# A hybrid residual block in one kernel: wider projections and attention outcome, fill without shared places, four gates moved to the dense stage

## The chip, the cores and the metric

The kernel runs on one core of a Trainium2 chip. The metric is the device time of one execution in microseconds (us): the median of three runs. TensorE is called PE here, VectorE DVE, ScalarE ACT, GpSimd POOL and SyncE SP.

## The reference

One layer on 1024 tokens of 1024 channels in float32. A normed input goes through one projection that is cut into an HGRN2 mixer (4 heads of 128), a forgetting attention (8 heads of 64), a cross attention into 256 memory tokens, and three sigmoid gates of 1024 channels. Each mixer is projected, gated and summed; an output projection and a residual follow, then a convolutional GLU.

```python
h = _rmsnorm(x, norm_mix_g[l])
z = h @ w_in[l]
(hq, hf, hi, hg, fq, fk, fv, ff, mq, gate_logits) = jnp.split(z, pts, axis=-1)
y_a = _hgrn2_mixer(hq, hf, hi, hg, lower_bounds[l], hgrn_norm_g[l])
y_b = _fox_mixer(fq, fk, fv, ff, fox_f_bias[l], fox_q_norm_g[l], fox_k_norm_g[l])
y_c = _memory_mixer(mq, mem_kv, mem_q_norm_g[l], mem_k_norm_g[l])
gates = jax.nn.sigmoid(gate_logits).reshape(B, T, N_BRANCH, D_MODEL)
merged = (gates[:, :, 0] * (y_a @ w_br_hgrn[l]) + gates[:, :, 1] * (y_b @ w_br_fox[l])
          + gates[:, :, 2] * (y_c @ w_br_mem[l]))
x = x + merged @ w_out[l]
x = x + _conv_glu_ffn(_rmsnorm(x, norm_ffn_g[l]), ffn_w_up[l], ffn_conv_w[l], ffn_conv_b[l], ffn_w_down[l])
```

The attention, for a block of 128 queries, with `Fc` the running sum of log forget gates (q and k are normed per head):

```python
s = (jnp.einsum('bhqd,bhkd->bhqk', qh[:, :, lo:hi], kh[:, :, :hi]) * scale
     + Fc[:, :, lo:hi, None] - Fc[:, :, None, :hi])
p = jax.nn.softmax(jnp.where(mask, s, -jnp.inf), axis=-1)
outs.append(jnp.einsum('bhqk,bhkd->bhqd', p, vh[:, :, :hi]))
```

## The kernel before

Every float32 operand of a dense product is split in a high and a low part: `split` (L166 and L174) casts to a rounded format on ACT (`wh`, `ph`) and subtracts on DVE (`wl`, `pl`), and `mm3` (L160 to L162) issues three matmuls: high with high, high with low, low with high.

The stages, in order of time in the profile. The first stage norms x and makes the first gates. The dense stage (to about 205 us) computes pairs of gates by a scheme of seven products instead of eight: 84 matmuls of 512 columns for each of 7 pairs, against 48 matmuls for a gate alone. `NCOVER`, `NPAIR` and `NFOX` say which gates of `ORDER` are made where: in the first stage, as pairs, or beside the attention. A gate goes out to `gd` in DRAM and comes back as `gt` where its branch is projected. Then come attention's values and the memory attention (to 318 us), the attention (to 680), HGRN with its first score matmul at 701, the branches (from about 880), the output projection, the up projection (from 1062) and the down projection (1490 to the end).

Attention, `fox_attn(p, i)`, takes head 2p+i. It loads the head's row of bias, spread over all partitions, into `nf` (one buffer, a DMA on SP). For each of eight tiles of 128 queries POOL makes a masked piece `nfm` (L919); PE makes scores `lg` (L924 and L925) in blocks of up to 512 keys; DVE adds the bias, leaves the sum in `pt` and the maximum in `st` (L930, and small steps on `st` at L935, L937 and L939); ACT takes the exponential (L940), DVE the reciprocal (L941), POOL normalises (L942). After every two tiles the outcome follows: PE transposes 128 by 128 pieces of both tiles into `tr` (L953 to L956, two banks), `split` makes `ph` and `pl`, and PE multiplies them with the split values `vhl` into `po` (L965 and L966), 256 columns wide. ACT and DVE add the halves of `po` (L969, L970) and SP stores them.

Beside it runs dense work, called the fill here: `fox_proj(p+1)` and `hgrn_values`, which call `token_major` with 256 columns (L160 to L162 with `pp<-wh,uh`, 256 columns), and ten gates (`gates_early`, `cm_chunk`, `pp<-uh,wh`, 512 columns). `weave` interleaves generators by their counts of steps, and `ahead` gives the attention's instructions a priority; the final order on each engine is set when the program is built, by a scheduler with a timeline of its own. Weights come as `raw` through SP, in `wp`, three buffers of each of `wh` and `wl`.

`hgrn_prep(h)` projects what a head of HGRN needs (`cm_chunk`, `gt` or `zt` at L1046, `ha`, `L`, `Gt`) and `hgrn_mix` starts from operands `kE`, `X` and `Xk`. `branch(br, yh, yl)` projects a mixer's output; before branch 0 eight DMAs on POOL's queue load the memory mixer's split output `yc`. At the start of the up projection the second norm's scale `rt` is made (sums on PE at L1416, a scalar step on DVE at L178, a power on POOL at L179) and spread by transposes (L366).

## Time and profile before

| what | value |
|---|---|
| median of 3 runs | 1699.6 us (1698.56 to 1700.24) |
| the profiled execution | 1700.23 us, its span 1698.4 us |
| mean granted PE clock | 0.999 |
| busy, PE / weight loads / DVE / ACT / POOL | 1691.0 / 1452.4 / 1150.8 / 800.9 / 324.6 us |
| instructions | 24291 |
| DMA | 227.16 MB, mean 134 GB/s |

A row of a group reads: line, engine, operation, out<-in, count, busy us, mean ns of one, and the idle time ahead of them with what ended it. A row of the timeline begins with the start and the busy time in us. PE's names `pp`, `lg`, `tr` and `po` stand for its banks of PSUM.

### The profile page before, as it was taken

The numbers are of one execution on the slowest core, as the hardware profiler recorded it, in microseconds if no ns is written. First come the engines' busy times: TensorE is split into PE (matmuls) and PEld (weight loads), VectorE is DVE, ScalarE is ACT, GpSimd is POOL, SyncE is SP. The second block draws the span as 40 slices with busy tenths as digits, with TensorE's granted clock in tenths as the row PEclk, the third lists the DMA queues.
The fourth block names the chain that finished last, engine by engine and source line by source line (L and its number), as shares of the span: only waits on it lengthen the run. The fifth ranks groups of instructions, "written<-read, shape, count | busy, mean of one in ns | idle before, by whom it ended". The sixth has DMA issues, their size and how long they took to land.

```text
span 1698.4 us, 24291 instructions
## 1 busy us (share of the span) xinstructions
PE 1691.0 (100%) x8957; PEld 1452.4 (86%) x8957; DVE 1150.8 (68%) x2057; ACT 800.9 (47%) x1428; POOL 324.6 (19%) x420
## 2 busy tenths in 40 slices
PE   9999999999999999999999999999999999999999
PEld 7888899989898998888888888888888888888887
DVE  6966455666666664886856845987878888775654
ACT  6734455545454553775631333644434444533432
POOL 0200032543433331544310000311111111100000
PEclk9999999999999999999999999999999999999999
DMA  9443232221212111110346542566544344494772
GB/s 367 157 161 106 88 139 68 77 92 51 94 59 77 63 46 57 67 32 13 106 127 209 167 186 100 165 174 169 158 139 138 118 149 143 172 363 145 251 269 87
DMA packets 83062, 227.16 MB, mean 134 GB/s; under 512 B 9712, under 2 KB 12408, under 8 KB 82816
## 3 DMA queue, kind: packets, MB, share of 16 engines
q1 hardware_dynamic: 64320, 160.54, 26.8%
q0 software_dynamic: 18048, 64.50, 13.2%
q8 instruction: 70, 1.15, 0.3%
q10 hardware_dynamic: 576, 0.59, 0.1%
q14 instruction: 48, 0.39, 0.1%
HBM read 180.72 MB, written 67.93 MB: 146 GB/s over the span
## 4 chain that ended last, share of the span: by engine, by line
PE 99%; DVE 0%; ACT 0%; DMA 0%; issue 0%; ACTq 0%; DVEq 0%
PE pp L160 21%; PE pp L162 21%; PE pp L161 21%; PE lg L160 4%; PE lg L162 4%; PE lg L161 4%; PE tr L162 3%; PE tr L161 3%; PE tr L160 3%; PE po L966 1%; PE lg L925 1%; PE lg L924 1%; PE po L965 1%; PE po L160 1%; PE po L161 1%; PE po L162 1%
## 5 line engine op out<-in xcount | busy, mean ns | idle before, releaser
L160 PE MATMUL pp<-uh,wh 128*128 128x512 f32 x412 | 163.3, 396 | 0.0
L161 PE MATMUL pp<-ul,wh 128*128 128x512 f32 x412 | 162.9, 395 | 0.0
L162 PE MATMUL pp<-uh,wl 128*128 128x512 f32 x412 | 162.5, 394 | 0.0
L161 PE MATMUL pp<-wl,uh 128*128 128x256 f32 (+1 forms) x512 | 146.3, 286 | 0.0
L162 PE MATMUL pp<-wh,ul 128*128 128x256 f32 (+1 forms) x512 | 146.1, 286 | 0.0
L160 PE MATMUL pp<-wh,uh 128*128 128x256 f32 (+1 forms) x512 | 145.6, 286 | 0.0
L166 ACT CAST wh<-s 128x512 fp32r<-128x512 f32 x110 | 66.5, 621 | 131.6 <-PE pp L161 55.1
L166 ACT CAST wh<-raw 128x1024 fp32r<-128x1024 f32 (+2 forms) x76 | 67.6, 890 | 100.6 <-PE pp L161 86.2
L166 ACT CAST wh<-rw 128x512 fp32r<-128x512 f32 x87 | 53.2, 619 | 108.1 <-PE pp L161 70.2
L160 PEld LDWEIGHTS pp<-wh,uh 128*128 128x128 f32 x512 | 97.3, 190 | 1.2
L161 PEld LDWEIGHTS pp<-wl,uh 128*128 128x128 f32 x512 | 97.4, 190 | 1.0
L162 PEld LDWEIGHTS pp<-wh,ul 128*128 128x128 f32 x512 | 97.4, 190 | 0.9
L1457 POOL DMA_DIRECT2D rw<-in_w_up x44 | 24.1, 555 | 372.4 <-DVE wl L1350 171.3
L166 ACT CAST dwh<-wr 128x1024 fp32r<-128x1024 f32 (+1 forms) x41 | 40.2, 980 | 115.8 <-PE tr L161 40.0
L162 PEld LDWEIGHTS pp<-uh,wl 128*128 128x128 f32 x412 | 77.5, 188 | 15.1
L174 DVE TENSOR_TENSOR wl<-raw,wh 128x1024 fp32r<-128x1024 f32 (+2 forms) x75 | 78.0, 1040 | 17.8 <-ACT wh L166 17.6
L160 PEld LDWEIGHTS pp<-uh,wh 128*128 128x128 f32 x412 | 77.5, 188 | 14.6
L161 PEld LDWEIGHTS pp<-ul,wh 128*128 128x128 f32 x412 | 77.5, 188 | 14.5
L940 ACT ACTIVATE pt<-pt,st 128x128 f32<-128x128 f32 (+3 forms) x64 | 49.7, 777 | 41.7 <-DVE st L937 33.9
L174 DVE TENSOR_TENSOR dwl<-wr,dwh 128x1024 fp32r<-128x1024 f32 (+1 forms) x41 | 46.3, 1129 | 31.7 <-ACT dwh L166 31.7
L942 POOL TENSOR_SCALAR pt<-pt,st 128x128 f32<-128x128 f32 (+3 forms) x64 | 49.1, 767 | 78.4 <-DVE st L941 64.1
L1350 DVE TENSOR_TENSOR wl<-rw,wh 128x512 fp32r<-128x512 f32 x69 | 47.7, 704 | 22.7 <-PE pp L162 18.2
(500 smaller groups left out, 5123.2 us busy)
## 6 DMA issues: line engine op xcount, KB each, us to landing
rw<-in_w_up POOLq DMA_DIRECT2D x44, 512.0 KB, 4.7
sd<-in_w_dn POOLq DMA_DIRECT2D x30, 512.0 KB, 6.0
br<-yd SPq DMA_DIRECT2D x30, 512.0 KB, 5.0
raw<-in_w_cm SPq DMA_DIRECT2D x24, 512.0 KB, 3.4
gd<-gt SPq DMA_DIRECT2D x48, 256.0 KB, 2.0
gt<-gd SPq DMA_DIRECT2D x48, 256.0 KB, 2.7
yd<-fc SPq DMA_DIRECT2D x44, 256.0 KB, 2.2
wr<-sd SPq DMA_DIRECT2D x20, 512.0 KB, 4.5
```

Source lines behind the costliest of these rows:

```text
L160: PE.matmul(ps, lh, rh, start=first, stop=False, skip_group_check=more)
L161: PE.matmul(ps, lh, rl, start=False, stop=False, skip_group_check=more)
L162: return PE.matmul(ps, ll, rh, start=False, stop=last, skip_group_check=more)
L166: return S.copy(out, in_)
L174: return (sub or V).tensor_sub(l, src, h.bitcast(F32))
L924: PE.matmul(ps[:, :w], qa[i][:, tsl], kh[i][:, s0:s0 + w], start=True, stop=False)
L925: fox_sets[p][3] = PE.matmul(ps[:, :w], qa[i][:, tsl], kl[i][:, s0:s0 + w], start=False, stop=True)
L940: S.activation(pt[:, :ns], pt[:, :ns], AF.Exp, bias=st[:, 2:3], accum_out=st[:, 3:4])
L942: G.tensor_scalar(pt[:, :ns], pt[:, :ns], st[:, 3:4], 0.0, ALU.mult, ALU.add)
L965: PE.matmul(o, vhl[:, sb, :], ph[:, src], start=(sb == 0), stop=False)
L1350: late["split"] = V.tensor_sub(l, src, h.bitcast(F32))
L1457: late["raw"] = G.dma_start(raw[:, 2 * i:2 * i + 2, :], src[:, 2 * i:2 * i + 2, :])
```

## The change

Nine parts:

1. `NPAIR` goes from 10 to 14: the dense stage makes nine pairs instead of seven, and the attention's fill six gates instead of ten.
2. The query-key projections of the last two head pairs become one of 512 columns (`fox_proj_late`), its result stored to `zd` in DRAM as it comes, and read back and normed by `fox_load`. HGRN's values become one projection of 512 columns as well, stored to `hid` and read back behind attention. The evacuation uses `gate_tile` in place of `Vf` and `z`.
3. The outcome takes groups of four tiles: four transposes fill a bank, and a matmul is up to 512 columns wide. Each tile's `pt` has its own place (`pt0` to `pt7`).
4. The addition of the last head's last `po` (`late["tail"]`) moves into `hgrn_prep(0)`.
5. The weave's counts of steps and what is woven with which head.
6. `wp` has four buffers instead of three (`WIDE`).
7. The loads of `yc` are spread over branch 0, each behind a small POOL instruction that waits for a gate's load.
8. The first unit of the up projection loads by SP; another part of it loads behind a mark on POOL.
9. The scratch for DMA descriptors is set to 2048 bytes.

```diff
-NCOVER, NPAIR = 2, 10
+NCOVER, NPAIR = 2, 14
-NFOX = [0, 3, 0, 3, 0, 3, 1]
+NFOX = 6
+WIDE = 4
...
-            hl = [wp.tile([P, 4 * 264], F32R, tag=t, name=t, bufs=3) for t in ("wh", "wl")]
+            hl = [wp.tile([P, 4 * 264], F32R, tag=t, name=t, bufs=WIDE) for t in ("wh", "wl")]
...
+    def fox_proj_late():
+        def evac(tb, ps):
+            t = gate_tile()
+            S.activation(t, ps, AF.Copy, scale=rt[:, tb:tb + 1])
+            SP.dma_start(zd[tb], t)
+        yield from token_major(w_late[0], HB, evac)
+
+    def fox_load(p):
+        cs = slice((p - 2) * 256, (p - 1) * 256)
+        for n in range(2):
+            z = fox_tile(p, n)
+            SP.dma_start(z, zd[4 * n:4 * n + 4, :, cs].rearrange("b p c -> p b c"))
+            fox_norm(z)
+            yield
...
-        for tp in range(4):
+        for g in range(2):
             pts = []
-            for j in range(2):
-                tb = 2 * tp + j
+            for tb in range(4 * g, 4 * g + 4):
...
-                pt = pf.tile([P, T], F32, tag="pt", name="pt", bufs=4)
+                pt = pf.tile([P, ns], F32, tag=f"pt{tb}", name=f"pt{tb}")
...
-            for sp in range(tp + 1):
+            for sb in range(4 * g + 4):
                 ptr = ps_tr()
...
+                first = max(sb - 4 * g, 0)
+                for j in range(first, 4):
+                    PE.transpose(ptr[:, j * P:(j + 1) * P], pts[j][:, sb * P:(sb + 1) * P], ident)
...
+                c = slice(first * P, HB)
+                split(S, ph[:, c], pl[:, c], ptr[:, c])
+                PE.matmul(po[:, c], vhl[:, sb, :], ph[:, c], start=sb == 0, stop=False)
+                PE.matmul(po[:, c], vhl[:, sb, :], pl[:, c], start=False, stop=sb == 4 * g + 3)
                 yield
...
+            if (h, g) == (7, 1):
+                late["tail"] = po, ybd[a, p, g * HB:(g + 1) * HB]
+                return
...
+    late_proj = fox_proj_late()
+    first = (fox_proj(1), chain(islice(late_proj, 4), fox_load(2)), gates_early(1))
+    second = (chain(gates_early(1), islice(late_proj, 4)), gates_early(2), gates_early(1))
     for p in range(3):
-        weave((ahead(fox_attn(p, 0), AHEAD), FOX_STEPS), (fox_proj(p + 1), 8))
+        weave((ahead(fox_attn(p, 0), AHEAD), FOX_STEPS), (first[p], (8, 6, 4)[p]))
         fox_prep(p + 1, fox_sets[p][3])
-        weave((ahead(fox_attn(p, 1), AHEAD), FOX_STEPS), (gates_early(NFOX[2 * p + 1]), 2 * NFOX[2 * p + 1], FOX_LATE))
+        weave((ahead(fox_attn(p, 1), AHEAD), FOX_STEPS), (second[p], 6, FOX_LATE),
+              *([(fox_load(3), 2, 0.1)] if p == 1 else []))
...
     for i in range(2):
-        weave((ahead(fox_attn(3, i), AHEAD), FOX_STEPS), (islice(values, 8), 8),
-              (gates_early(0 if i else NFOX[6]), 2 * NFOX[6], FOX_LATE))
+        weave((ahead(fox_attn(3, i), AHEAD), FOX_STEPS), (chain(gates_early(1 - i), islice(values, 4)), 6 - 2 * i))
...
-    run_all(hgrn_prep(0))
+    for i, _ in enumerate(hgrn_prep(0)):
+        if i == 2:
+            fox_out(gate_tile()[:64, :], *late.pop("tail"))
...
-    for c in range(4):
-        for t, d in zip(yc, ycd):
-            with tc.issue_after(state["norm"].ins):
-                G.dma_start(t[c], d[:, c, :].bitcast(F32R))
-    run_all(branch(0, yh, yl))
+    for i, _ in enumerate(first_branch):
+        if i % 3 and i < 12:
+            p, c = i % 3 - 1, i // 3
+            mark = G.tensor_scalar(warm, late["gates"][:, 0:1], 1.0, 0.0, ALU.mult, ALU.add)
+            with tc.issue_after(mark.ins):
+                G.dma_start(yc[p][c], ycd[p][:, c, :].bitcast(F32R))
...
-            late["raw"] = G.dma_start(raw[:, 2 * i:2 * i + 2, :], src[:, 2 * i:2 * i + 2, :])
+            with tc.issue_after(late["pool"].ins) if after else nullcontext():
+                late["raw"] = (SP if begun else G).dma_start(raw[:, 2 * i:2 * i + 2, :], src[:, 2 * i:2 * i + 2, :])
...
-    nc = bacc.Bacc("TRN2", target_bir_lowering=False, num_devices=1)
+    nc = bacc.Bacc("TRN2", target_bir_lowering=False, num_devices=1, dynamic_dma_scratch_size=2048)
```

Line numbers move: L160 to L162 of before are L161 to L163 of the new program, the scores L954 and L955, the transposes L980, the outcome L985 and L986.

The change moves instructions on every engine. The first place is the end of attention on PE, before: the last outcome group of head 7 (`po`) with the rows around it; `pp` is a dense product.

```order
L966 MATMUL po<-pl,vhl 128x256
L965 MATMUL po<-ph,vhl 128x256
L966 MATMUL po<-pl,vhl 128x256
L953 MATMUL tr<-ident,pt 128x128 x2
L954 MATMUL tr<-ident,pt 128x128 x2
L953 MATMUL tr<-ident,pt 128x128
L956 MATMUL tr<-ident,pt 128x128
L954 MATMUL tr<-ident,pt 128x128
L965 MATMUL po<-ph,vhl 128x256
L966 MATMUL po<-pl,vhl 128x256
L965 MATMUL po<-ph,vhl 128x256
L966 MATMUL po<-pl,vhl 128x256
```

Some twenty rows of `pp` stand ahead of these, and twenty more between them and the last `po` rows. In the new program the same place, from the last scores of head 7 (`lg`, of its eighth tile) to the first transposes of its second group of four tiles:

```order
L954 MATMUL lg<-kh_3_5661,qa_3_5663 128x512
L955 MATMUL lg<-kl_3_5665,qa_3_5663 128x512
L980 MATMUL tr<-ident,pt_6545 128x128
L980 MATMUL tr<-ident,pt_6558 128x128
L985 MATMUL po<-ph,vhl 128x512
L986 MATMUL po<-pl,vhl 128x512
L985 MATMUL po<-ph,vhl 128x384
L980 MATMUL tr<-ident,pt_6558 128x128
L986 MATMUL po<-pl,vhl 128x384
L985 MATMUL po<-ph,vhl 128x256
L986 MATMUL po<-pl,vhl 128x256
L980 MATMUL tr<-ident,pt_6642 128x128
```

No `pp` row stands there, nor anywhere between the first transposes of head 5's first group and the last `po` of head 7; all of the fill stands ahead.

The second place is DVE's queue at the end of attention. Before, with `gt<-pp` and `wl<-raw` the fill's work:

```order
L174 TENSOR_TENSOR pl<-tr,ph 128x384
L1046 TENSOR_TENSOR gt<-pp,rx 128x512
L970 TENSOR_TENSOR yp<-po,yp 64x256
L174 TENSOR_TENSOR pl<-tr,ph 128x512 x2
L174 TENSOR_TENSOR wl<-raw,wh 128x1024
L174 TENSOR_TENSOR pl<-tr,ph 128x512
L174 TENSOR_TENSOR pl<-tr,ph 128x384
L970 TENSOR_TENSOR yp<-po,yp 64x256
```

In the new program:

```order
L929 TENSOR_TENSOR yp<-po,yp 64x512
L175 TENSOR_TENSOR pl<-tr,ph 128x512 x5
L175 TENSOR_TENSOR pl<-tr,ph 128x384
L175 TENSOR_TENSOR pl<-tr,ph 128x256
L175 TENSOR_TENSOR pl<-tr,ph 128x128
L1074 TENSOR_TENSOR gt<-pp,rx 128x512
```

The last splits of attention now stand without the fill's work between them, and the evacuation of a dense product that PE has done earlier (`gt<-pp`) stands behind them all.

The third place is the start of the up projection on PE. Before, the transposes that spread `rt` stand behind the products of `B22` and `T3`:

```order
L161 MATMUL pp<-T3l_10857,wh_10869 128x512
L162 MATMUL pp<-T3h_10856,wl_10870 128x512
L366 MATMUL tr<-ident,rt_10790 128x128 x8
L160 MATMUL pp<-B11h_10175,wh_11004 128x512
L161 MATMUL pp<-B11l_10176,wh_11004 128x512
```

In the new program:

```order
L162 MATMUL pp<-T2l_9746,wh 128x512
L163 MATMUL pp<-T2h_9745,wl_10333 128x512
L161 MATMUL lg<-B22h_10420,wh_10337 128x512
L367 MATMUL tr<-ident,rt_10356 128x128 x8
L162 MATMUL lg<-B22l_10421,wh_10337 128x512
```

They have moved up to behind the first matmul of `B22`, seven matmuls behind the sums from which `rt` is made.

More of the change, by code (lines that the diff above doesn't have):

```diff
@@ L577, in operand @@
             if self.half is None:
-                self.half = [wp.tile([P, 4 * 264], F32R, tag=t, name=t, bufs=3) for t in ("wh", "wl")]
+                self.half = [wp.tile([P, 4 * 264], F32R, tag=t, name=t, bufs=WIDE) for t in ("wh", "wl")]
                 h, l = (t[:, :HB] for t in self.half)
@@ L706, in token_major @@
         with tc.issue_after(late["load"].ins):
-            w = [weights(src[q], (4, ncol)) for q in range(2)]
+            per = 2 if ncol == HB else 4
+            w = [weights(src[q], (per, ncol)) for q in range(KC // per)]
         for tb in range(8):
@@ L1287, in branch @@
                 gts.append(gt)
+            late["gates"] = gts[0]
             for n, ps in br_chunk(br, j, yh, yl):
@@ L1360, in first_operands @@
         a11, a21, a22, a12 = raw
-        h = [wp.tile([P, 4 * 264], F32R, tag="wh", name="wh", bufs=3) for _ in range(2)]
-        sums = [wp.tile([P, 4 * 264], F32R, tag="wl", name="sums", bufs=3).bitcast(F32) for _ in range(2)]
+        h = [wp.tile([P, 4 * 264], F32R, tag="wh", name="wh", bufs=WIDE) for _ in range(2)]
+        sums = [wp.tile([P, 4 * 264], F32R, tag="wl", name="sums", bufs=WIDE).bitcast(F32) for _ in range(2)]
         s1, s2, s4 = sums[0][:, :HB], sums[0][:, HB:2 * HB], sums[1][:, :HB]
@@ L1504, in families @@
                 for k in range(4):
-                    late["last"] = family_block(name, k, quarters(k)[q], G if name == "B21" and k > 1 else None)
+                    sub = G if name == "B21" and k > 1 else None
+                    late["pool" if sub else "last"] = family_block(name, k, quarters(k)[q], sub)
             if name == "T3":
@@ L1776, in pieces @@
         return out
[L1778 removed]
     o["w_fqk"] = c(np.stack([pieces(np.concatenate([fk[:, p * P:(p + 1) * P], fq[:, p * P:(p + 1) * P]], axis=1),
[L1780 removed]
+                                    [(0, 256)])[0] for p in range(2)]))
+    late = np.concatenate([m[:, p * P:(p + 1) * P] for p in (2, 3) for m in (fk, fq)], axis=1)
+    o["w_late"] = c(np.stack([kmaj(m).reshape(P, 4, 2 * HB).transpose(1, 0, 2) for m in (late, hi)]))
     pv = pieces(np.concatenate([fv, ff], axis=1), [(0, 256), (256, 520)])
```

83 lines of the change are left out of this document (38 added, 45 removed).

## The prediction

> **What bounds the kernel now.** I read the page's busy line and its chain first, then PE's waits, then busy time by window, then single groups and the timeline around the places that the change touches.
>
> ```profile
> span 1698.4 us, 24291 instructions
> PE 1691.0 (100%) x8957; PEld 1452.4 (86%) x8957; DVE 1150.8 (68%) x2057; ACT 800.9 (47%) x1428; POOL 324.6 (19%) x420
> PE 99%; DVE 0%; ACT 0%; DMA 0%; issue 0%; ACTq 0%; DVEq 0%
> PE lg L160 <- ACT uh L349: 1.8, 1, 1.8
> PE tr L265 <- POOL dull L263: 1.0, 1, 1.0
> PE po L1189 <- DVE St L1195: 0.7, 1, 0.7
> PE pp L162 <- DVE wl L1350: 0.2, 1, 0.2
> ```
>
> PE is busy throughout, is 99% of the chain, and waits four times in the whole program, 3.7 us together, mostly at the start. So every matmul removed is time gained, and every wait that PE newly meets is time lost; nothing else counts. The profiled execution took 1700.2 us (1.8 us outside its span), 0.6 us over the median of 1699.6. A difference of 0.2%, 3.4 us, is about what a measurement of this kernel can tell from none.
>
> The columns of the next rows are the window in us, then busy time and count of PE, weight loads, DVE, ACT and POOL, then the granted clock, DMA share and GB/s.
>
> ```profile
> 5.00:10.00 5.00, 3.70 (x10) 2.76 (x11) 4.46 (x12) 3.48 (x8) 0.00 (x0) 0.73 1.04 395
> 100.00:200.00 100.00, 100.00 (x443) 82.81 (x442) 51.91 (x82) 38.51 (x68) 3.94 (x8) 1.00 0.27 95
> 600.00:680.00 80.00, 80.00 (x538) 73.39 (x537) 43.06 (x140) 35.52 (x72) 19.27 (x30) 1.00 0.17 54
> ```
>
> 100 to 200 is the dense stage of gate pairs, 600 to 680 the end of attention. There DVE has 43 us of work in 80 because dense matmuls (the fill) stand between attention's own. That is the cover at stake.
>
> **PE's work.** The pitch of a matmul, start to start, is read from runs of equal ones in the timeline:
>
> ```profile
> 1201.63 0.39 PE L160 MATMUL pp<-T4h,wh 128*128 128x512 f32 x1
> ...
> 1202.99 0.39 PE L160 MATMUL pp<-T4h,wh 128*128 128x512 f32 x1
> 599.80 0.28 PE L160 MATMUL pp<-wh,uh 128*128 128x256 f32 x1
> ...
> 601.00 0.28 PE L161 MATMUL pp<-wl,uh 128*128 128x256 f32 x1
> ```
>
> Six steps in 1.36 us give 0.227 us for 512 columns, ten in 1.20 give 0.120 for 256. One wide matmul is thus 0.013 us cheaper than two narrow ones. By instruction counts of both programs the change takes away 992 matmuls of 256 columns and 32 of 128, and adds 456 of 512 and 32 of 384. With 0.17 for 384 (an estimate, halfway between the two pitches) and 0.09 for 128 (an estimate, below the 0.120): -992 x 0.1195 = -118.5, +456 x 0.2267 = +103.4, +32 x 0.17 = +5.5, -32 x 0.09 = -2.9, in all **-12.5 us**. By part: four gates leave the fill with 48 matmuls each and come back as two pairs of 84 in the dense stage, 24 x 0.227 = -5.4; the late query-key and HGRN-value projections go from 768 narrow to 384 wide, -4.7; the outcome matmuls of eight heads are the other 2.4.
>
> The Trainium skill, "TensorE: Matmul & The Clock Gate", section "Back-to-back issue gap", gives an isolated matmul 262 cycles for 256 columns and 518 for 512 at 2.4 GHz, so that widening would save 2.5 ns on a pair. By it the 384 pairs of the projections give 1 us and not 4.7. The trace shows 13 ns on a pair, so I keep 4.7.
>
> **The fill, and what is left bare.** Beside attention, from its first scores to its last outcome matmul, before has 868 narrow and 611 wide fill matmuls: 868 x 0.1195 + 611 x 0.2267 = 242 us. The new program has 105 and 816: 198 us. What decides is where they stand. In PE's new order no fill row stands behind the first transposes of head 5's outcome: its transposes and outcome, and most of heads 6 and 7, follow bare, 224 matmuls, 108 of them transposes of 0.108, 72 outcome and 44 score matmuls; at these pitches 33.0 us. In before, fill stands to the last outcome group. So for these 33 us PE moves as fast as the softmax does, whose work goes on DVE:
>
> ```profile
> L174 DVE TENSOR_TENSOR pl<-tr,ph 128x512 fp32r<-128x512 f32 x48 | 32.2, 684 | 12.0 <-ACT ph L166 11.8
> L174 DVE TENSOR_TENSOR pl<-tr,ph 128x384 fp32r<-128x384 f32 x32 | 17.6, 549 | 1.4 <-ACT ph L166 1.3
> L930 DVE CUSTOM_DVE_ANT_0 pt<-lg,nf 128x512 f32<-128x512 f32 x32 | 22.0, 689 | 20.8 <-PE lg L925 10.8 <-PE tr L953 9.7
> L930 DVE CUSTOM_DVE_ANT_0 pt<-lg,nf 128x384 f32<-128x384 f32 x16 | 8.8, 552 | 1.5 <-PE lg L925 1.4
> L930 DVE CUSTOM_DVE_ANT_0 pt<-lg,nf 128x256 f32<-128x256 f32 x16 | 6.7, 418 | 5.4 <-PE tr L953 4.0 <-PE lg L925 1.3
> L930 DVE CUSTOM_DVE_ANT_0 pt<-lg,nfm 128x128 f32<-128x128 f32 x64 | 18.2, 285 | 13.2 <-POOL nfm L919 7.0 <-PE lg L925 2.8 <-PE po L965 2.0
> L930 DVE DVE_READ_ACCUMULATOR2_ANT st<- 128x1 f32 x144 | 11.8, 82 | 0.0
> L937 DVE TENSOR_SCALAR st<-st 128x1 f32<-128x1 f32 x56 | 11.6, 207 | 0.8
> L941 DVE RECIPROCAL st<-st 128x1 f32<-128x1 f32 x64 | 10.3, 160 | 27.4 <-ACT pt L940 26.8
> L970 DVE TENSOR_TENSOR yp<-po,yp 64x256 f32<-64x256 f32 x32 | 13.2, 412 | 13.1 <-ACT yp L969 12.9
> 655.26 0.55 DVE L930 CUSTOM_DVE_ANT_0 pt<-lg,nf 128x384 f32<-128x384 f32 x1
> 655.73 0.09 DVE L930 DVE_READ_ACCUMULATOR2_ANT st<- 128x1 f32 x1
> 655.73 0.29 DVE L930 CUSTOM_DVE_ANT_0 pt<-lg,nfm 128x128 f32<-128x128 f32 x1
> ```
>
> DVE has 145 instructions in the bare stretch. Those that weigh: 18 splits of 512 (12.3), 6 of 384 (3.3), 12 narrower ones (5.0), the masked sums with maximum (8 x 0.69, 4 x 0.55, 4 x 0.42, 17 x 0.285: 14.2), 33 accumulator reads (2.7), 36 small steps (6.7), 5 additions of the outcome and one value split (2.7): 47 us. The last three rows show that a following instruction starts some 0.08 us ahead of the end of the one before, and that an accumulator read costs nothing of its own; 33 x 0.08 for the reads and about 100 x 0.08 for the rest leave 36.5. So the new wait has a floor of 36.5 - 33 = 3.5, with 1.5 at the entry **5 us**, and 47 - 33 = **14 us** where nothing overlaps.
>
> Neither bound counts latencies. At the last tile of a head (1024 columns) the chain of before runs so:
>
> ```profile
> 658.34 0.21 DVE L937 TENSOR_SCALAR st<-st 128x1 f32<-128x1 f32 x1
> 658.65 1.15 ACT L940 ACTIVATE pt<-pt,st 128x1024 f32<-128x1024 f32 x1 [1.71 <-DVE st L937]
> 659.70 0.18 ACT L940 ACTIVATION_READ_ACCUMULATOR pt<-pt,st 128x1 f32 x1
> 659.92 0.16 DVE L941 RECIPROCAL st<-st 128x1 f32<-128x1 f32 x1 [1.37 <-ACT pt L940]
> 660.25 1.12 POOL L942 TENSOR_SCALAR pt<-pt,st 128x1024 f32<-128x1024 f32 x1 [6.18 <-PE tr L956]
> L166 ACT CAST ph<-tr 128x512 fp32r<-128x512 f32 x48 | 27.1, 588 | 24.9 <-PE tr L954 16.9 <-PE po L965 7.4
> nf<-negFd SPq DMA_DIRECT2D x8, 512.0 KB, 3.7
> ```
>
> That is 3.0 us from the maximum to the normalised tile; ahead of it lie the last scores' latency (0.3), two sums (0.55 and 0.29) and the three-way maximum (0.19), and in the new DVE order two splits and two small steps of the outcome of the group before (1.3): 5.7, with hops between engines about 6.5 us. PE's new order leaves 2.2 us of work (head 6) and 2.7 (head 7) between those scores and the transposes that need the tile, where before never leaves under 6.7. So two waits of about 4 us, **8 us**. The other waits are in the loop over key blocks: two transpose banks go round in 0.32 + 0.26 (latency) + 0.59 (cast) + 0.68 (split) + 0.13 = 2.0 us, against 2 x (4 x 0.108 + 2 x 0.227) = 1.77 of PE, and DVE does sums in between; and a head's first tile waits for the reload of its one row buffer, 3.7 us by the last row. I followed both queues by hand with these durations, each instruction from the latest of its queue, its data and its bank: PE is late by 1.5 us at head 5's second group, 3.9 at head 6's first, 8.1 at its second, 11.1 at head 7's first, 15.2 at its second, 17.8 at the end. Between 14 and 17.8 I take **16 us**, bounds 5 and 25 (half again on the walk).
>
> **Behind attention.**
>
> ```profile
> 694.65 0.68 DVE L1166 TENSOR_TENSOR kE<-kE,kt 128x512 f32<-128x512 f32 x1
> 698.87 0.68 DVE L1098 TENSOR_TENSOR X<-X,hq 128x512 f32<-128x512 f32 x1
> 701.01 0.89 PE lg L1102 x8
> ```
>
> The last outcome matmul of before is at 679.7. HGRN's first operand is ready at 695.3, 15.6 us later; PE had 17.5 us of fill for it, and has 12.2 in the new order: about **+3 us** (0 if the chain starts earlier beside the bare stretch, 5 if DVE is late with the fill's own results).
>
> At the start of the up projection the second norm's transposes move from behind two products to behind the first matmul of one:
>
> ```profile
> 1069.83 0.95 PE L1416 MATMUL po<-ones,r 128*128 128x1 f32 x8
> 1071.46 0.16 DVE L178 TENSOR_SCALAR rt<-po 128x8 f32<-128x8 f32 x1
> 1071.70 2.65 POOL L179 TENSOR_TENSOR rt<-rt,mhalf 128x8 f32<-128x8 f32 x1 [2.63 <-DVE rt L178]
> ```
>
> They need POOL's power, ready 3.6 us behind the sums and 3.0 where DVE takes its step 0.6 sooner, as its new order allows, with 1.6 us of PE ahead of them (7 matmuls): a wait of 1.4 to 2.0 us. Before loses some 0.65 us in short gaps of this unit behind its later transposes, which may fall away. I take **+1 us**, bounds 0 and 2.
>
> **At nothing**: the two more pairs (DVE has 48 us free in 100 of the dense stage); the round trips of projections and HGRN values through DRAM (one store per token block on SP, read back a head later; uncovered, about 4 us each, as the row reload); the memory operand's loads, spread over the first branch behind marks on POOL (all issued over 13 us before use); the fourth weight buffer; the smaller descriptor scratch; the first unit's loads moved from POOL's to SP's queue.
>
> Sum: 1700.2 - 12.5 + 16 + 3 + 1 = 1707.7; less the 0.6 to the median, **1707 us**, a loss of 0.4%.
>
> **Rivals.** (a) *The cover is enough*: DVE runs near its floor and HGRN's chain overlaps the bare stretch: 1699.6 - 12.5 + 5 + 1 = 1693 us, and 1687 with no wait at all. For it: DVE is only 54% busy at 600 to 680 and before shows no wait of PE there. Against: that stretch had fill. It decides below 9.1 us of new waits. Chance 0.2. (b) *Waits and saving cancel*, 9 to 16 us together, around 1699: 0.16. (c) *Latencies are worse than the walk*, 25 + 4 + 2 of waits: 1718: 0.17. (d) *The clock falls*: the second row of windows' table, 5 to 10 us, has a granted clock of 0.73 behind the start's short burst and a 1.8 us wait; waits of 4 us could bring such a clock back. With three of them followed by 5 us at 0.73, 3 x 5 x 0.37 = 5.5 us more, 1713. Against: only the start shows it. The same page, section "The HAM clock gate", puts a drop to half at an idle window of some 3.4 us; no wait of this trace is that long. Chance 0.07. The forecast's own case, 1703 to 1712, has 0.4.
>
> **Numbers.** Faster by over 0.2%: 0.2 (a). Within: 0.16 (b). Slower: 0.64 (forecast, c, d). The range leaves out the best part of (a) and the worst of (c): 1693 to 1719; the forecast's own range is 1703 to 1712.
>
> **What would show it.** Right: PE's waits between the last fill and HGRN's first matmuls, naming DVE's splits, POOL's normalised tiles and the row reload, 14 to 18 us, one of 3 to 4 us at each last tile; DVE above 75% there; matmul count down by 536. Wrong: fewer than 6 us of waits there, DVE near its floor and the time below 1696; or waits elsewhere, in the dense stage or at the second branch's first matmul, where I put none.

## The result and the profile after

| | before | after |
|---|---|---|
| median | 1699.83 us (5 runs) | 1716.13 us (5 runs, 1714.90 to 1716.77) |
| the profiled execution | 1700.23 us, span 1698.4 | 1715.19 us, span 1713.4 |
| ratio | | 1.0097, 95% interval 1.0083 to 1.0110 |

The kernel became 16.3 us slower where 7.4 were forecast: the sign was right, and the forecast less than half of the size. The page of the new kernel begins, and its chain reads:

```profile
span 1713.4 us, 23255 instructions
PE 1690.1 (99%) x8421; PEld 1422.7 (83%) x8421; DVE 1167.5 (68%) x2089; ACT 803.3 (47%) x1436; POOL 329.9 (19%) x430
PE 95%; DVE 2%; ACT 1%; DMA 1%; issue 0%; POOL 0%; ACTq 0%; SPq 0%; POOLq 0%; DVEq 0%
```

536 matmuls are gone, and PE is busy for only 0.9 us less than before. Six of PE's waits, in us together, times, and the longest:

```profile
PE tr L980 <- POOL pt L972: 3.3, 2, 1.7
PE lg L954 <- DVE st L960: 2.8, 4, 1.1
PE tr L162 <- DVE B21l L175: 1.6, 1, 1.6
PE tr L980 <- DVE pl L175: 1.3, 1, 1.3
PE pp L161 <- ACT wh L167: 1.2, 1, 1.2
PE tr L367 <- POOL rt L180: 0.7, 1, 0.7
```

All of PE's waits together are some 19 us, against 3.7 before. That is less than what was lost. More of it is in the windows, with the columns of the prediction's (the granted clock stands behind POOL's busy time):

```profile
660.00:665.00 5.00, 3.27 (x11) 2.52 (x12) 3.61 (x17) 2.18 (x7) 2.59 (x6) 0.58 0.79 289
665.00:670.00 5.00, 5.00 (x25) 4.28 (x24) 3.58 (x15) 3.25 (x10) 1.84 (x5) 0.74 0.00 0
680.00:685.00 5.00, 3.15 (x10) 2.02 (x10) 1.97 (x3) 1.48 (x3) 2.05 (x3) 0.63 0.27 66
685.00:690.00 5.00, 5.00 (x23) 3.79 (x21) 2.63 (x4) 2.45 (x5) 0.00 (x0) 0.69 0.13 42
```

At the last tiles of heads 6 and 7 the clock falls, and PE is then "busy" with slow matmuls. The timeline at the first of the two places:

```profile
658.35 0.62 PE L980 MATMUL tr<-ident,pt 128*128 128x128 f32 x4
659.43 1.12 POOL L972 TENSOR_SCALAR pt<-pt,st 128x1024 f32<-128x1024 f32 x1 [1.10 <-DVE st L971]
660.61 0.53 PE L980 MATMUL tr<-ident,pt 128*128 128x128 f32 x2 [1.63 <-POOL pt L972]
662.26 0.69 PE L954 MATMUL lg<-kh,qa 128*128 128x384 f32 x1 [1.12 <-DVE st L960]
663.06 0.63 PE L985 MATMUL po<-ph,vhl 128*128 128x512 f32 x1
663.49 0.63 PE L986 MATMUL po<-pl,vhl 128*128 128x512 f32 x1
```

The transposes wait 1.6 us for the normalised tile, the chain that the prediction named; the next scores 1.1 us; and behind that a matmul of 512 columns has a pitch of 0.43 us where it had 0.227. Narrower windows show when the clock fell:

```profile
660.00:660.80 0.80, 0.20 (x2) 0.20 (x2) 0.65 (x1) 0.12 (x1) 0.55 (x1) 1.00 0.76 220
661.20:662.20 1.00, 0.00 (x0) 0.00 (x0) 0.30 (x3) 0.90 (x2) 0.45 (x1) 0.50 1.04 391
679.60:681.30 1.70, 0.04 (x1) 0.00 (x0) 0.85 (x2) 0.78 (x3) 1.14 (x2) 1.00 0.00 0
681.30:682.50 1.20, 0.69 (x2) 0.29 (x2) 0.00 (x0) 0.60 (x2) 0.91 (x2) 0.50 0.26 60
```

At both places it goes to half at the end of one wait, of 1.6 and 1.7 us; the wait of 1.1 us comes behind the first fall. PE's busy time in the four windows of 5 us times what the clock lacks (3.27 x 0.42 + 5 x 0.26 + 3.15 x 0.37 + 5 x 0.31) gives **5.4 us**, an estimate of what the lowered clock cost.

Where the time went is read from the starts of four rows: attention's first scores, HGRN's last product with the state, the sums of the second norm, and the last matmul. Before, then after:

```profile
326.69 0.40 PE L924 MATMUL lg<-kh,qa 128*128 128x128 f32 x2
881.64 0.39 PE L1189 MATMUL po<-St,qe 128*128 128x128 f32 x2
1067.54 0.95 PE L1416 MATMUL po<-ones,r 128*128 128x1 f32 x8
1694.40 0.39 PE L162 MATMUL po<-dbh,dwl 128*128 128x512 f32 x1
```
```profile
362.61 0.48 PE L954 MATMUL lg<-kh,qa 128*128 128x128 f32 x2
891.26 0.39 PE L1217 MATMUL po<-St,qe 128*128 128x128 f32 x2
1077.40 0.95 PE L1450 MATMUL po<-ones,r 128*128 128x1 f32 x8
1709.01 0.39 PE L163 MATMUL po<-dbh,dwl 128*128 128x512 f32 x1
```

From the first to the second (attention and HGRN) before takes 554.95 us. Four gates have left it (4 x 48 x 0.2267 = 43.5) and wider matmuls save 7.1, so 504.35 would be left; it takes 528.65: **24.3 us lost**. Nearly all of it lies in the bare stretch, from the last fill matmul to the last outcome matmul:

```profile
635.60:691.00 55.40, 44.81 (x225) 33.12 (x223) 40.84 (x153) 33.63 (x75) 20.65 (x35) 0.88 0.24 77
```

Its 224 matmuls take 55.4 us, where the prediction's pitches give 33.0: 22.4 us. From the third to the fourth it takes 631.61 for 626.86: **4.75 us lost**. Between the second row and the third lie 185.9 us before and 186.1 after, so nothing was lost there. The two losses, of the attention stage and of the up projection, are given for the experiments below, worked out in the same way. In the kernels of numbers 6, 8 and 9, and in `e11`, 14 matmuls of the first branch stand behind the second row instead of ahead of it, so 3.2 us (14 x 0.2267) are added to their loss in the attention stage. The losses leave out the first microseconds of the program, in which PE's clock rises and which differ by some 2 us from run to run.

In the up projection the waits are for `B21l` and for weights, 3.5 us of the 4.75 with that for `rt`. PE's three, and the loads of the first two units, in the new kernel; then the loads before:

```profile
1083.02 2.05 PE L367 MATMUL tr<-ident,rt 128*128 128x128 f32 x16 [0.68 <-POOL rt L180]
1092.14 0.50 PE L162 MATMUL tr<-B21l,wh 128*128 128x512 f32 x1 [1.58 <-DVE B21l L175]
1096.12 0.50 PE L161 MATMUL pp<-B11h,wh 128*128 128x512 f32 x1 [1.19 <-ACT wh L167]
1073.36 1.06 SPq L1492 DMA_DIRECT2D rw<-in_w_up  x2
1090.88 1.16 POOL L1492 DMA_DIRECT2D rw<-in_w_up  x2
```
```profile
1053.27 1.06 POOL L1457 DMA_DIRECT2D rw<-in_w_up  x2 [163.03 <-ACT sqs L1392]
1068.02 1.05 POOL L1457 DMA_DIRECT2D rw<-in_w_up  x2 [13.69 <-ACT B22h L166]
```

Against the sums, the first load is issued 4 us ahead instead of 14, and the second 13.5 us behind instead of 0.5.

### The profile page after: what moved, and what is told of

It is laid out like the page before. It is cut to its first block, busy times and chain, and to the rows that moved or that the text cites. A ratio compares the mean times of both kernels' runs of the same rounds, so it can differ in the third digit from the quotient of the medians.

```text
span 1713.4 us, 23255 instructions
## 1 busy us (share of the span) xinstructions
PE 1690.1 (99%) x8421; PEld 1422.7 (83%) x8421; DVE 1167.5 (68%) x2089; ACT 803.3 (47%) x1436; POOL 329.9 (19%) x430
## 4 chain that ended last, share of the span: by engine, by line
PE 95%; DVE 2%; ACT 1%; DMA 1%; issue 0%; POOL 0%; ACTq 0%; SPq 0%; POOLq 0%; DVEq 0%
PE pp L163 20%; PE pp L161 20%; PE pp L162 20%; PE lg L161 5%; PE lg L163 5%; PE lg L162 5%; PE tr L161 3%; PE tr L162 3%; PE tr L163 3%; PE tr L980 2%; PE po L986 1%; PE po L161 1%; PE po L985 1%; PE po L163 1%; PE po L162 1%; PE lg L955 1%
## 5 line engine op out<-in xcount | busy, mean ns | idle before, releaser
L161 PE MATMUL pp<-uh,wh 128*128 128x512 f32 x356 | 141.1, 396 | 1.1 <-DVE gt L1074 1.1
L163 PE MATMUL pp<-uh,wl 128*128 128x512 f32 x356 | 140.8, 395 | 0.0
L162 PE MATMUL pp<-ul,wh 128*128 128x512 f32 x356 | 140.6, 395 | 0.0
L162 PE MATMUL pp<-wl,uh 128*128 128x256 f32 (+2 forms) x384 | 123.8, 323 | 0.0
L161 PE MATMUL pp<-wh,uh 128*128 128x256 f32 (+2 forms) x384 | 123.6, 322 | 0.0
L163 PE MATMUL pp<-wh,ul 128*128 128x256 f32 (+2 forms) x384 | 123.3, 322 | 0.0
L161 PEld LDWEIGHTS pp<-uh,wh 128*128 128x128 f32 x356 | 67.0, 188 | 14.2 <-DVE gt L1074 1.3
L163 PEld LDWEIGHTS pp<-uh,wl 128*128 128x128 f32 x356 | 67.0, 188 | 13.2
L162 PEld LDWEIGHTS pp<-ul,wh 128*128 128x128 f32 x356 | 67.0, 188 | 12.6
L163 PEld LDWEIGHTS pp<-wh,ul 128*128 128x128 f32 x384 | 72.9, 190 | 5.2
L162 PEld LDWEIGHTS pp<-wl,uh 128*128 128x128 f32 x384 | 72.9, 190 | 4.9
L161 PEld LDWEIGHTS pp<-wh,uh 128*128 128x128 f32 x384 | 72.8, 190 | 4.9
L167 ACT CAST ph<-tr 128x512 fp32r<-128x512 f32 (+1 forms) x96 | 43.5, 478 | 51.0 <-PE tr L980 47.8
L175 DVE TENSOR_TENSOR pl<-tr,ph 128x512 fp32r<-128x512 f32 (+1 forms) x96 | 51.1, 551 | 22.1 <-ACT ph L167 20.8
```

The lines of the kernel that those rows point to most:

```text
L161: PE.matmul(ps, lh, rh, start=first, stop=False, skip_group_check=more)
L162: PE.matmul(ps, lh, rl, start=False, stop=False, skip_group_check=more)
L163: return PE.matmul(ps, ll, rh, start=False, stop=last, skip_group_check=more)
L167: return S.copy(out, in_)
L175: return (sub or V).tensor_sub(l, src, h.bitcast(F32))
```

## The experiments

Each was timed against the kernel before on the same chip (1700.0 to 1700.6 us). "Held" means that `mm3` gets this, so that a dense matmul stays behind the scores that stand ahead of it in the program:

```diff
+        with tc.issue_after(late["hold"].ins) if late.get("hold") else nullcontext():
             PE.matmul(ps, lh, rh, start=first, stop=False, skip_group_check=more)
...
                     fox_sets[p][3] = PE.matmul(ps[:, :w], qa[i][:, tsl], kl[i][:, s0:s0 + w], start=False, stop=True)
+                    if p == 3:
+                        late["hold"] = fox_sets[p][3]
```

**1. Fill of the last pair held** (`e1_hold`, the diff above).

> Same instructions as the changed kernel; only the fill of the last head pair (one gate, HGRN's values, the first HGRN head's projections) may not be issued by PE before the scores of attention that stand ahead of it in the program, so that it stands between the transposes and outcome matmuls of heads 6 and 7. If the bare end is the cause, the waits there (about 15 us) and the low clock (about 6 us) go, less some 3 to 5 us of new waits: 1697 to 1703 us. If the four-tile groups themselves are too slow for PE wherever the fill stands, the waits move with the fill and the time stays above 1710.

1731.92 us, ratio 1.0189 (1.0174 to 1.0204). The end of attention is covered without a gap, and the wait has moved to the start of the last pair, whose preparation had lost its cover; attention stage 40.3 us lost:

```profile
PE lg L955 <- DVE qa L917: 9.3, 2, 5.3
PE tr L983 <- DVE kl L911: 5.5, 2, 3.6
```

Both expectations missed: covering one place laid another bare.

**2. Transposes that do no useful work in the two holes** (`e2_dull`).

```diff
+                if h > 5 and g and sb == 0:
+                    for _ in range(16):
+                        PE.transpose(ptr[:, 0:P], ident, ident)
```

> Adds 16 transposes of the identity (3.5 us of PE in all for two heads) ahead of the first transposes of the second group of heads 6 and 7, where PE idles; they do no useful work. If idle time of PE lowers its granted clock, the clock stays at 1.00 there and the time falls by 4 to 6 us, to 1710 to 1712, with the waits on the softmax unchanged. If the slow matmuls have another cause, the clock stays near 0.6 to 0.7 and the time is 1716 to 1719.

1718.54 us, 1.0108 (1.0093 to 1.0123). The clock stays at 1.00 at both holes:

```profile
660.00:665.00 5.00, 3.86 (x29) 3.14 (x28) 1.43 (x5) 2.96 (x6) 2.04 (x2) 1.00 0.86 296
680.00:685.00 5.00, 3.71 (x28) 2.98 (x28) 1.75 (x5) 3.51 (x8) 3.56 (x5) 1.00 0.03 7
685.00:690.00 5.00, 4.77 (x23) 4.02 (x22) 2.35 (x5) 1.76 (x3) 0.00 (x0) 0.66 0.36 98
```

So at these holes it is idle time that lowers it, and a busy PE keeps it up. But it falls 5 us further on, and the time is not better (attention stage 26.2 us lost). Without the 3.5 us of the added transposes and the later low clock (4.77 x 0.34 = 1.6) that is 21.1, so the clock at the two holes was worth some 3 us here and not 5.4: part of the time that it costs is spent waiting anyway.

**3. Four gates back in the fill** (`e4_pair10`): `NPAIR` 10, `NFOX` 10, the gates spread over the weaves.

> The four gates are back in attention's fill (seven pairs), the rest as changed. PE has 5.4 us more work and 43 us more fill; the fill now reaches further, and about 100 matmuls (some 15 us) stay bare instead of 224. If the amount of fill decides, the loss at attention's end falls from 21 to about 8 us: 1706 to 1710. If only the placement decides and not the amount, it is as long as now or longer: 1715 to 1722.

1711.00 us, 1.0065 (1.0050 to 1.0080). With 43.5 us more fill the stage loses 13.6 us instead of 24.3; the rest is still lost at a bare end. Slightly above the range for "the amount decides": it does, but not alone.

**4. HGRN's values in place again** (`e6_vf`).

```diff
-            t = gate_tile()
-            S.activation(t, ps, AF.Copy, scale=rt[:, tb:tb + 1])
-            SP.dma_start(hid[tb], t)
+            S.activation(Vf[:, tb, :], ps, AF.Copy, scale=rt[:, tb:tb + 1])
```

> HGRN's values (still 512 columns wide) are written straight into the attention's value tile again, so that they wait for the split values of the last heads; no store to DRAM and no read back. PE's order then has 110 matmuls of fill among the last 150 rows of attention. If the freeing of this place let the fill run early and left the end bare, the waits and the low clock there go: 17 to 21 us less, 1695 to 1699. If the four-tile groups are too slow with fill beside them as well, or fill is now missing earlier, as when it was held from head 6 on (1732), more than 1708.

1719.23 us, 1.0107 (1.0093 to 1.0122); stage 26.9 us lost. PE's order had the fill at the end, and the bare stretch now lay at heads 4 to 6 (560 to 620 us). My theory that the freed place was the cause fell with it. `e8_vf_pad`, which adds the tile of number 7:

> Both: values written in place and the up projection's pools moved. If the two causes are separate and add up: 1691 to 1695 us, 5 to 9 below the kernel before. If they share a cause, as far down as the better of the two alone.

1720.45 us, 1.0116 (1.0099 to 1.0133): no sum of two gains, since neither was one.

**5. The four gates moved alone, in the kernel before** (`e7_before_14`).

```diff
-NCOVER, NPAIR = 2, 10
+NCOVER, NPAIR = 2, 14
-NFOX = [0, 3, 0, 3, 0, 3, 1]
+NFOX = [0, 2, 0, 1, 0, 2, 1]
```

> The kernel before with the four gates moved alone: nine pairs in the dense stage, six gates in the fill (none, two, one, two and one beside heads 1, 3, 5 and the last pair). If only the number of matmuls counts and the fill still reaches the end (its order shows 89 fill matmuls among the last 150 rows), 24 matmuls fewer: 1700 - 5.4 = 1694 to 1696. If less fill means waits, 1698 to 1706.

1722.75 us, 1.0129 (1.0113 to 1.0144), though PE has 5.4 us less work: the stage loses 29.1 us. Each head's matmuls at the pitches above against the time that the head took put 14 us of it at head 2, which keeps 4 us of fill, 4 each at heads 3 and 5, and 6 behind the last head. The longest wait, 3.4 us, is this one, and the clock falls behind it as well:

```profile
PE lg L924 <- DVE st L930: 4.1, 4, 3.4
```

Together with number 3 this says that taking 43.5 us of fill away is enough to lose more than the pairs save, with the old narrow groups too. The up projection loses nothing here (626.8 us from the sums to the end), so that loss belongs to another part.

**6. The same work, spread over all heads** (`e10_spread`: held for all heads, one gate moved; `e12_spread_b`: held from head 1, gates moved once more; both change the weave's counts as well. The diff is that of the second, its first two lines against the hold of number 1, the others against the changed kernel).

```diff
-                    if p == 3:
+                    if h >= 1:
...
-    first = (fox_proj(1), chain(islice(late_proj, 4), fox_load(2)), gates_early(1))
-    second = (chain(gates_early(1), islice(late_proj, 4)), gates_early(2), gates_early(1))
+    first = (fox_proj(1), chain(islice(late_proj, 4), fox_load(2)), gates_early(2))
+    second = (islice(late_proj, 4), gates_early(2), gates_early(1))
...
-        weave((ahead(fox_attn(p, 1), AHEAD), FOX_STEPS), (second[p], 6, FOX_LATE),
+        weave((ahead(fox_attn(p, 1), AHEAD), FOX_STEPS), (second[p], (4, 4, 2)[p], 0.0),
```

> The work of the changed kernel, but each dense matmul that stands in the program beside attention is kept behind the scores that stand ahead of it, for all heads, and one gate moves from beside head 1 to beside head 5. By PE's order the fill between successive heads' last outcome matmuls is then 38, 23, 16, 16, 16, 27, 25 and 32 us, never under 28% of a stretch of 12 us, where the changed kernel has 41, 44, 29, 44, 27, 12, 0 and 0. If waits come from stretches without fill alone, wherever they lie, 15 to 20 us go: 1697 to 1702. If 198 us of fill are too few for attention however they lie, waits are spread as well: 1708 or more.

1716.70 us, 1.0097 (1.0082 to 1.0112), stage 26.5 lost (a projection of 10 us moves behind the first scores, so the wait ahead of them counts in it). The end was covered and HGRN began 8 us sooner, but holding head 0's fill bared the preparation ahead of the first scores:

```profile
PE tr L905 <- DVE z L857: 7.4, 1, 7.4
```

> As the spread fill before, but head 0's fill isn't held, so that the first head's preparation keeps its cover (that run lost 7.4 us there), and the gates stand so that the fill between last outcome matmuls is 27, 23, 16, 22, 16, 22, 27 and 32 us. If the loss is a matter of where the fill lies, 1700 to 1705. If 198 us are too few for groups of four tiles, wherever they lie, waits stay at the heads with 16 us: 1708 to 1714.

1710.59 us, 1.0061 (1.0046 to 1.0076), stage **18.1** lost. Same instructions, 6.2 us less lost than in the changed kernel: placement is worth that much, and is not all. Worked out by head as in number 5, 6 us are lost in head 0, 5 in head 2, 3 each in heads 1 and 3, and none in head 4, though heads 2 and 4 both have 16 us of fill and head 0 has 27. So the waits did not stay at the heads with 16 us, as expected for too little fill: the amount of a head's fill alone does not say what it loses.

**7. The up projection's start.** `e3_up_old`: the loads as before the change.

```diff
-            with tc.issue_after(late["pool"].ins) if after else nullcontext():
-                late["raw"] = (SP if begun else G).dma_start(raw[:, 2 * i:2 * i + 2, :], src[:, 2 * i:2 * i + 2, :])
+            late["raw"] = G.dma_start(raw[:, 2 * i:2 * i + 2, :], src[:, 2 * i:2 * i + 2, :])
```

> The first unit of the up projection loads by POOL's queue again and no load waits for a mark on POOL. If these loads cause the 4.7 us lost at the start of the up projection, they go: 1711 to 1713. If the loss comes from the moved transposes of the norm's scale and the order of ACT's and DVE's work there, nothing changes: 1715 to 1717.

1718.22 us, 1.0110 (1.0093 to 1.0127); up projection 5.7 us lost. The first load, on POOL's queue again, is issued only 5.5 us behind the sums. `e5_pad`: an unused tile below its pools, which restores ACT's order there.

```diff
+    pad = tc.alloc_tile_pool(name="pad", bufs=1, side="left")
+    pad.tile([P, 2 * 1056], F32, tag="pad", name="pad")
     pw = Rounded(tc, name="pw", bufs=1, side="left", reuse_waits="tile")
```

> An unused tile of 8448 bytes moves the up projection's pools to the places where they would not lie on weight buffers still in use; with it ACT casts B22 ahead of the first product's copy again, as before the change, and the transposes of the scale stand behind all of B22. If the fourth weight buffer, by its place under those pools, makes the 4.7 us at the start of the up projection, 3.5 to 4.7 go: 1711 to 1713 us. If the loss has another cause, 1716.

1718.66 us, 1.0106 (1.0091 to 1.0121); 6.4 us lost. The first load was now issued 4.6 us behind the sums, where it is 4.0 ahead in the changed kernel, and the weights came late. Both edits together, `e9_pad_up_old`:

> The unused tile of 8448 bytes and the old loads together: PE's, ACT's and DVE's order at the start of the up projection is then that of the kernel before. If that start is lost to both at once (loads on SP's queue come late where the place is mended, B21's low parts come late where it is not), 4 to 5 us go: 1711 to 1714. If the earlier stages hand over something that is late in itself, 1716 to 1719.

1718.75 us, 1.0108 (1.0093 to 1.0123); 7.1 us lost, with the order on PE, ACT and DVE of the kernel before: the first loads are issued at 1084.4 us, 5.1 us behind the sums, after a wait for PE. Order alone isn't the cause. `e14_swap` changes the load's place in memory by allocating `pf2` ahead of `pw`, with the old loads:

> The changed kernel with the up projection's two pools allocated in the other order and the loads on POOL's queue, so that its weight tiles no longer lie on weight buffers in use: if late loads by their place cause the 4.7 us there, 4 to 5 go: 1711 to 1713. If not, 1716 to 1719.

1715.59 us, 1.0093 (1.0076 to 1.0110): loads 13 us ahead of the sums. `e3`, which differs from this kernel in the order of the pools alone, has them 5.5 behind, so their place decides when they go. Still 4.3 us are lost. What was late now was POOL's share of `B21l`, two subtractions that took 8.5 us, 7.2 the first and 1.3 the second, as in this row of number 8's second kernel:

```profile
1076.81 8.46 POOL L176 TENSOR_TENSOR B21l<-x,B21h 128x512 fp32r<-128x512 f32 x2 [0.65 <-ACT B21h L168]
```

PE waited 1.8 us for it in `e14`, and behind the wait the granted clock was 0.57 (1094 to 1096 us). With the swap, the old loads and `B21l` all on DVE (the last two kernels of number 8) 1.0 us is lost. `B21l` all on DVE without the swap was not tried. `e11_spread_pad_up_old`, a spread with the edits of `e9_pad_up_old`, showed only that the two stages' losses are separate:

> The two before together. If both causes are right and separate: 1692 to 1697 us, faster than the kernel before by 0.2 to 0.5%. If only one of them is right: 1697 to 1712.

1718.05 us, 1.0106 (1.0089 to 1.0123); 26.1 and 7.3 us lost.

**8. Seven pairs, spread** (ten gates in the fill again; by the trace 227 us of it stand ahead of the last outcome matmul, and not 241): `e13_spread_pair10` (held from head 1).

> Four gates back in the fill (seven pairs), held and spread in the same way: 241 us of fill as before, no head with under 24.7 us. PE has 7 us less work than the kernel before. If amount and placement together decide, attention has next to no waits and what is left is the start of the up projection: 1697 to 1700. If four-tile groups are slow in themselves, above 1704.

1707.45 us, 1.0044 (1.0029 to 1.0059), stage 9.9 lost, 6 of it in head 0. That is above the 1704 that was put on groups slow in themselves, but `e18` below has the same groups at 1698.4. With swapped pools and old loads, `e15_spread_pair10_swap`:

> The last two together: if both causes hold, 1692 to 1696, some 5 us faster than the kernel before; if one of them, 1697 to 1704.

1706.56 us, 1.0038 (1.0024 to 1.0051), 9.1 and 3.1 lost. Held from head 2 only, one more gate at head 0, `B21l` on DVE, `e16_spread_pair10_c`:

> As the last of the spread kernels (seven pairs, swapped pools, old loads), but fill is held only from head 2 on, so that head 0's first groups have 42 us of fill again (that kernel lost 5 us there), and B21's low parts are all made by DVE, where POOL took 4.2 us for each of its two. If both waits go: 1706.6 - 5 - 2 = 1699 to 1701. If they only move: 1704 to 1707.

1706.64 us, 1.0039 (1.0025 to 1.0053), 11.4 and 1.0 lost. The up projection was mended; in attention one wait of 6 us came up, and the timeline shows the round trip through DRAM in it. The read back of `z` is issued at 398.16, ACT's square of it stands in ACT's queue and waits for it, and the transposes wait behind the preparation that comes next on ACT; behind it the granted clock is 0.50 (402 to 408 us):

```profile
398.16 0.37 SPq L889 DMA_DIRECT2D z<-zd  x1
401.77 0.63 ACT L854 ACTIVATE fsq<-z 128x512 f32<-128x512 f32 x1 [3.48 <-DMA z<-zd]
403.00 0.68 ACT L910 ACTIVATE kh<-tr,cv 64x512 fp32r<-64x512 f32 x1
404.62 1.73 PE L983 MATMUL tr<-ident,pt 128*128 128x128 f32 x7 [6.04 <-DVE kl L911]
```

Held from head 1 again, so that this projection doesn't run ahead, `e18_spread_pair10_d` (against the changed kernel; with `mm3` as in the first diff):

```diff
-NCOVER, NPAIR = 2, 14
+NCOVER, NPAIR = 2, 10
-NFOX = 6
+NFOX = 10
...
+                    if h >= 1:
+                        late["hold"] = fox_sets[p][3]
...
-    first = (fox_proj(1), chain(islice(late_proj, 4), fox_load(2)), gates_early(1))
-    second = (chain(gates_early(1), islice(late_proj, 4)), gates_early(2), gates_early(1))
+    first = (chain(fox_proj(1), gates_early(1)), chain(islice(late_proj, 4), fox_load(2), gates_early(1)), gates_early(3))
+    second = (islice(late_proj, 4), gates_early(2), gates_early(2))
...
-        weave((ahead(fox_attn(p, 0), AHEAD), FOX_STEPS), (first[p], (8, 6, 4)[p]))
+        weave((ahead(fox_attn(p, 0), AHEAD), FOX_STEPS), (first[p], (10, 8, 6)[p]))
...
-        weave((ahead(fox_attn(p, 1), AHEAD), FOX_STEPS), (second[p], 6, FOX_LATE),
+        weave((ahead(fox_attn(p, 1), AHEAD), FOX_STEPS), (second[p], (4, 4, 4)[p], 0.0),
...
-    pw = Rounded(tc, name="pw", bufs=1, side="left", reuse_waits="tile")
     pf2 = Rounded(tc, name="pf2", bufs=1, side="left", reuse_waits="tile")
+    pw = Rounded(tc, name="pw", bufs=1, side="left", reuse_waits="tile")
...
-            with tc.issue_after(late["pool"].ins) if after else nullcontext():
-                late["raw"] = (SP if begun else G).dma_start(raw[:, 2 * i:2 * i + 2, :], src[:, 2 * i:2 * i + 2, :])
+            late["raw"] = G.dma_start(raw[:, 2 * i:2 * i + 2, :], src[:, 2 * i:2 * i + 2, :])
...
-                    sub = G if name == "B21" and k > 1 else None
+                    sub = None
```

> Seven pairs, swapped pools, old loads, B21's low parts all on DVE, and fill held from head 1 on, so that the projection that makes a round trip through DRAM doesn't run ahead and its norm doesn't stand in ACT's queue while it loads (6 us in the kernel before this one); head 0 gets one more gate, 34 us of fill between first scores and last outcome matmul instead of 27. If the round trip and head 0's want of fill are what is left: 1698 to 1702. If each such arrangement only moves the wait: 1704 to 1707.

**1698.44 us** (11 runs, 1697.60 to 1699.37) beside 1700.45: ratio 0.9989 (0.9980 to 0.9998), the only version that is not slower than the kernel before, by 2 us or 0.1%. The stage loses 3.8 us and the up projection 1.0, so most of the 7.1 us that PE saves in it is still lost. PE's longest waits:

```profile
span 1696.7 us, 23286 instructions
PE lg L162 <- ACT uh L351: 1.6, 1, 1.6
PE po L989 <- DVE pl L176: 1.5, 2, 0.8
PE tr L267 <- POOL dull L265: 1.0, 1, 1.0
PE tr L368 <- POOL rt L181: 0.7, 1, 0.7
```

In the attention stage PE waits 1.7 us in all, against 0.7 before; where the other 2.8 us of the 3.8 go is not shown.

**9. Groups of two tiles, spread** (`e17_two_tiles_spread`): the outcome as before the change, otherwise as `e12_spread_b`.

> As the second spread run (nine pairs, fill held from head 1, gates in the same places), but attention's outcome in groups of two tiles of 256 columns again, which gives PE 2.4 us more work. If groups of four tiles need more cover than groups of two (the last tile's chain is waited for by four tiles' transposes), 5 to 8 us of waits go and the time is 1704 to 1708. If the group's size does not matter, 1712 to 1714.

1744.48 us, 1.0270 (1.0255 to 1.0285), stage 47.8 us lost. It does not speak for the rival that groups of four tiles need more cover; but most of its waits lie at the preparations of pairs, which the hold had bared, so it does not settle what a group's size costs.

## Why the prediction was right or wrong, point by point

- **PE's work, -12.5 us**: as counted, 536 matmuls fewer. With the two losses, -12.5 + 24.3 + 4.75 = 16.6; less 1.7 us by which PE's start happened to be shorter in the profiled run this is 14.9, and between the spans lie 15.0.
- **The bare end, 16 us, and HGRN's start, 3 us**: place and mechanism right. The bare end lost 22.4 us; without the 5.4 estimated for the lowered clock, 17.0 are left, or some 19 with the 3 us that number 2 puts on the clock: near the 17.8 of the walk by hand and the 16 that I took. Some 2 us are left for HGRN's start. The waits at the two last tiles name POOL's normalised tile, as forecast, though 1.6 and 1.7 us and not 4, with others close by.
- **The clock**: the first step that failed. I put it at a chance of 0.07, outside the sum, because no wait of the trace of before was as long as 3.4 us, and priced it at 5.5 us. It came, at an estimated 5.4 (3 by number 2), behind waits of 1.6 and 1.7 us. The prediction's own row of 5 to 10 us (the first of its table) had the low clock behind a wait of 1.8. The Trainium skill, "TensorE: Matmul & The Clock Gate", section "The HAM clock gate (the "warmup" mystery)", has the clock at half after an idle window of some 3.4 us; here it went to half at the end of a single wait of half that length, and the measurement decides.
- **The up projection, +1 us**: the second step that failed. The wait of the moved transposes was there and small (0.7 us). I had put the loads that moved to SP, the mark on POOL and the fourth weight buffer at nothing; the loads came 10 and 13 us later against the sums, and 4.75 us were lost. That the place of the loads' tiles in memory decides when they are issued is shown by `e3` beside `e14`; that early loads are not enough is shown by `e14` itself, which lost 4.3 us until DVE made all of `B21l` (1.0). Which of the buffer, the queue and the mark costs how much alone is not shown; a kernel with three buffers and the rest of the change was not tried.
- **At nothing, the round trips through DRAM**: right in the changed kernel, where none is waited for; wrong as soon as the projection runs ahead: in `e16` ACT waits 3.5 us for the data, near the 4 us that the prediction gave for an uncovered one, and PE 6.0 us behind it.
- **Rivals**: "the cover is enough" was wrong by its own point: 29 us of waits and slow clock where it needed under 9. The sum of the forecast's case and of (d) is 1713, and with the up projection's 4.75 for 1 it is 1716. Rival (c), 1718, came as near in number, but by luck: it takes 25 us of latencies at the bare end, where the waits were near those of the walk and the clock made the rest.
- **Cause**: that the fill stands early and the end is bare was shown in the profile; that moving it to the end cures it fell with `e1` and `e6`. What the runs show is that attention lives on its cover: 43.5 us of fill taken away cost the kernel before 29.1 us of waits and clock (`e7`), given back to the new kernel they save 10.7 (`e4`), a better spread 6.2 (`e12`), both 20.5 (`e18`). So amount and place both count. What a head needs is not shown, since head 4 of `e12` loses nothing with 16 us and its head 0 loses 6 with 27, and whether a spread exists in which 198 us are enough is open.

## What to carry to other kernels

Work that leaves a covered stage takes its cover along: price it not by its own time but by the chain of the stage that it hid, here 29 us of new losses for 5.4 us of matmuls saved. When a matmul engine that was never idle begins to wait, count the lowered clock behind the waits as well. And look where the next stage's first loads come to lie: the order in which two pools are allocated moved their issue by 18 us here (`e3`, `e14`).

## What the runs showed of the hardware

- **One wait of 1.6 us can lower the clock.** Behind waits of 1.6 and 1.7 us the granted clock was 0.50, and a matmul of 512 columns took 0.43 us for some 7 us; 16 small transposes in the hole kept it at 1.00 there. A wait of 1.58 us in the up projection of the same run (to 1092.1 us) left it at 1.00, so the length of the wait alone doesn't decide.
- **The start differs by run.** In the first 10 us the new kernel and its variants with the same matmuls differ by up to 2 us, in which matmuls of 512 columns have a pitch of 0.43 us for longer.
- **POOL's and DVE's subtractions hold each other up.** On POOL 128x512 took 1.3 to 1.7 us in the kernels before and after, while DVE's beside it took up to 1.8 instead of 0.69. In `e14` and `e15` the first of POOL's two took 7.2 us while DVE made ten without a break beside it, at 0.69 each, and the second 1.3. The 4.2 us that an expectation above gives for each is their mean. The Trainium skill, "SBUF — State Buffer", section "SBUF: two separate sides", has the two engines share a pair of ports with an exclusive lock; the trace agrees with that, the 7.2 us of the one and the 1.8 of the other beside it. Four such subtractions on DVE alone took 2.5 us:

```profile
1075.35 2.49 DVE L176 TENSOR_TENSOR B21l<-x,B21h 128x512 fp32r<-128x512 f32 x4
```
